# Gate and value products of a conv-FFN by seven Strassen products, residual added by DMA

## The chip, the cores and the metric

The kernel runs on one core of one Trainium2 chip. The metric is the time of one execution on the device, in microseconds. Five engines work side by side, each from its own instruction queue: TensorE (PE in the profile, with PEld for its weight loads), VectorE (DVE), ScalarE (ACT), GpSimd (POOL) and SyncE (SP), which here only issues DMAs. Matmuls read their operands from SBUF and write PSUM; DVE and ACT bring PSUM back into SBUF.

## The reference

One transformer layer on 512 latent tokens and 256 context tokens, model width 2048. Two attention mixers, a residual, and then the channel mixer, which is what the change touches:

```python
def _conv_ffn(h, w_up, conv_w, conv_b, w_down):
    g, u = jnp.split(h @ w_up, 2, axis=-1)
    T = g.shape[1]
    pad = CONV_W // 2
    gp = jnp.pad(g, ((0, 0), (pad, pad), (0, 0)))
    g = sum(gp[:, j:j + T] * conv_w[j] for j in range(CONV_W)) + conv_b
    return (jax.nn.silu(g) * u) @ w_down
...
        x = x + g1 * (_merge_heads(o_da, o_mla, subln_w[l], lambda_init) @ w_o[l])

        h2 = _modulate(_rmsnorm(x, norm2_w[l]), sh2, s2)
        x = x + g2 * _conv_ffn(h2, w_up[l], conv_w[l], conv_b[l], w_down[l])
...
    return _rmsnorm(x, final_w)
```

`w_up` is 2048 x 11264 (gate and value, 5632 columns each), `w_down` 5632 x 2048. Everything is float32; the convolution runs over three neighbouring tokens.

## The kernel before

Tensors lie transposed: features on the 128 partitions, tokens along the free dimension. A float32 product is made of three matmuls in the fast `float32r` format: each operand is split into a high part (a cast on ACT, L75) and a low part (a subtraction on DVE, L76), and `mm3` (L96) multiplies high by high, high by low and low by high (L99, L100, L101), all added up in PSUM. `wblock` (L82) loads a 128 x 1024 block of weights (512 KB, issued by SP, three buffers) and splits it, also into three buffers each for the high and the low part.

The order of the work on each engine is set by a planner: it walks the program with modelled costs, and on each engine issues the earliest instruction of the program whose inputs it takes as ready. So a later instruction may stand ahead of an earlier one that still waits. The engines then run their queues strictly in that order.

The channel mixer comes after the output projection, whose last part builds `x1`, the residual stream, as 16 tiles of 128 features x 512 tokens (L700). `token_norm` (L666) gives the reciprocal root mean square, and a loop over the 16 tiles (L710 to L717) normalises, modulates and splits them into `hx`, 16 pairs of a high and a low tile.

The 5632 gate columns make 44 tiles of 128, and so do the value columns. A *pair* here is one gate tile with the value tile of the same number; its result is 128 x 512 tokens each, for 16 k-tiles of 128.

- `first_pair` computes pairs 0 and 1 together (L723), so that each normalised tile can be used as soon as it is ready: 16 k-tiles x 4 outputs x 3 matmuls of 512 columns. Its four outputs fill both `s` tiles of PSUM (each 128 x 1024, two banks).
- `up(ft)` computes one pair in one `s` tile (L736): four weight blocks of 8 k-tiles each, 96 matmuls of 512 columns.
- `activate` (L747) takes the gate through the convolution (one ACT operation with the middle weight and the bias, two DVE operations for the neighbours), SiLU on ACT, the product with the value on DVE, and the split of the result.
- `down` (L762) multiplies four activation tiles (a *chunk*) with `w_down`: eight weight blocks, 16 output tiles of 12 matmuls each in `b` tiles of PSUM (four of one bank), and DVE multiplies each output by its modulation and adds it to `x1` in SBUF (L771).

The eleven chunks run in this order: pairs of chunk c, then down of chunk c - 1. The last down runs in two halves of 256 tokens, because the final norm of the first half can start while PE works on the second. The final norm and the stores of the output end the kernel.

Of the kernel before, what the change touches and what calls it, by code (L numbers as in the profile page):

```python
# [9 lines left out]
F32 = mybir.dt.float32  # L10
F32R = mybir.dt.float32r
BF16 = mybir.dt.bfloat16
AF = mybir.ActivationFunctionType
# [4 lines left out]
P = 128  # L18
# [31 lines left out]
def layer_kernel(ctx: ExitStack, tc: tile.TileContext, small, rope, c_row, cc_row, x_t, ctx_t, ada, ada_k,  # L50
# [51 lines left out]


    sm = ctx.enter_context(tc.tile_pool(name="sm", bufs=1))
    sm.tile([P, 96], F32, name="edge")
    rim = ctx.enter_context(tc.tile_pool(name="rim", bufs=1, side="right"))
    rim.tile([P, 120], F32, name="rim")


    smt = cst.tile([P, NSMALL], F32, name="smt")  # L110
# [2 lines left out]
    def col(name, j=0):  # L113
        o = OFF[name] + j
        return smt[:, o:o + 1]

    ropet = cst.tile([P, 2, T], F32, name="ropet")
# [14 lines left out]
    q0_d = dram.tile([2, P, T], F32, name="q0_d")  # L132
    cq_d = [dram.tile([2, P, T], F32, name=f"cq_d{i}") for i in range(3)]
    ckv_d = [dram.tile([2, P, TT], F32, name=f"ckv_d{i}") for i in range(2)]
    o_d = [dram.tile([P, T], F32, name=f"o_d{h}") for h in range(NH)]
    kr_d = dram.tile([2, P, TT], F32, name="kr_d")
    k_d = [dram.tile([2, P, TT], F32, name=f"k_d{h}") for h in range(NH)]
# [32 lines left out]
    def a2k(dt=F32):  # L170
        return ap_.tile([P, 512], dt, tag="a2k", name=nm("a2k"))
# [423 lines left out]
    mb = None  # L595
    nxt = latent_pair(0)
    da.release()
    bp = ctx.enter_context(tc.tile_pool(name="bp", bufs=16, reuse_waits="tile"))

    def b2k(dt=F32):  # L600
        return bp.tile([P, 512], dt, tag="b2k", name=nm("b2k"))
# [38 lines left out]
    mb.release()  # L640
    ma.release()
    mc.release()
    ps_b.release()
    ps_b = ctx.enter_context(tc.tile_pool(name="ps_c", bufs=4, space=PSUM, reuse_waits="tile"))


    ap_ = tc.alloc_tile_pool(name="ap2", bufs=32, side="right", reuse_waits="tile")
    wo = tc.alloc_tile_pool(name="wo", bufs=1, reuse_waits="tile")
    cb = wo.tile([P, D], F32, name="cb2")
# [16 lines left out]
    def token_norm(pool, ss, last):  # L666

        n = ss.shape[1]
        po = b_tile()[:, :n]
        pe.matmul(po, ones32, ss, start=True, stop=False)  # L670
        for i, x in enumerate(last):
            q = pool.tile([P, T], F32, tag="sq", name=nm("sq"), bufs=2)[:, :n]
            sc.square(q, x)
            pe.matmul(po, ones32, q, start=False, stop=i == len(last) - 1)
        r, t1, t2 = (pool.tile([P, T], F32, tag=g, name=nm(g), bufs=1)[:, :n] for g in ("nr", "n1", "n2"))
        rstd(r, po, D, t1, t2)
        return r

# [29 lines left out]
    r = token_norm(wo, ss, x1[12:])  # L708
    hx = []
    for dt in range(KT):  # L710
        t = wo.tile([P, T], F32, tag="xr", name=nm("xn"), bufs=3)
        ve.tensor_tensor(t, x1[dt], r, op=ALU.mult)
        h = wo.tile([P, T], F32, tag="h", name=nm("h"), bufs=2)
        sc.activation(h, t, AF.Identity, scale=a2[:, dt:dt + 1], bias=modx[:, 48 + dt:49 + dt])
        hl = a2k(F32R), a2k(F32R)
        split(hl[0], hl[1], h)
        hx.append(hl)  # L717
    wo.release()


    ff = tc.alloc_tile_pool(name="ff", bufs=1, reuse_waits="tile")

    def first_pair():  # L723
# [12 lines left out]
    def up(ft):  # L736
        s = s_tile()
        for i in range(2):
            o = s[:, i * 512:(i + 1) * 512]
            for hf in range(2):  # L740
                wh, wl = wblock(w_up[ft - 2, i, hf])
                for j in range(8):
                    kt = hf * 8 + j
                    mm3(o, (wh[:, j * P:(j + 1) * P], wl[:, j * P:(j + 1) * P]), hx[kt], kt == 0, kt == KT - 1)
        return activate(ft, s)

    def activate(ft, s):  # L747
        g, u = s[:, :512], s[:, 512:]
        t = ff.tile([P, T], F32, tag="t", name=nm("t"), bufs=2)
        sc.activation(t, g, AF.Identity, scale=col("cw", NFT + ft), bias=col("cb", ft))  # L750
        ve.scalar_tensor_tensor(out=t[:, 1:], in0=g[:, :T - 1], scalar=col("cw", ft), in1=t[:, 1:],
                                op0=ALU.mult, op1=ALU.add)
        ve.scalar_tensor_tensor(out=t[:, :T - 1], in0=g[:, 1:], scalar=col("cw", 2 * NFT + ft), in1=t[:, :T - 1],
                                op0=ALU.mult, op1=ALU.add)
        sc.activation(t, t, AF.Silu)
        a = ff.tile([P, T], F32, tag="sq", name=nm("a"), bufs=2)
        ve.tensor_tensor(a, t, u, op=ALU.mult)
        hl = [ff.tile([P, T], F32R, tag=g_, name=nm(g_), bufs=6) for g_ in ("ah", "al")]
        split(hl[0], hl[1], a)
        return hl  # L760

    def down(c, acts, ts=slice(0, T), then=None):  # L762
        for dp in range(8):
            wh, wl = wblock(w_dn[c, dp])
            for i in range(2):
                dt = dp * 2 + i
                po = b_tile()[:, :ts.stop - ts.start]
# [3 lines left out]
                ve.scalar_tensor_tensor(out=x1[dt][:, ts], in0=po, scalar=modx[:, 80 + dt:81 + dt],  # L771
                                        in1=x1[dt][:, ts], op0=ALU.mult, op1=ALU.add)
                if then:
                    then(dt)

    acts = first_pair() + [up(ft) for ft in range(2, FC)]
    for c in range(1, NFC):
        nxt = [up(c * FC + f) for f in range(FC)]
        down(c - 1, acts)
        acts = nxt  # L780


    norms = []
    for th in range(2):
        ts = slice(th * 256, (th + 1) * 256)
        ss = ff.tile([P, 256], F32, tag="ss", name=nm("ss"), bufs=2)
        down(NFC - 1, acts, ts, lambda dt: add_square(ff, ss, x1[dt][:, ts], dt == 0) if dt < 12 else None)
        norms.append(ss)
    exp_ln_tables()
    for th in range(2):  # L790
        ts = slice(th * 256, (th + 1) * 256)
        r = token_norm(ff, norms[th], [x[:, ts] for x in x1[12:]])
        for dt in range(KT):
            y = a2k()[:, :256]
            ve.scalar_tensor_tensor(out=y, in0=x1[dt][:, ts], scalar=col("fw", dt), in1=r, op0=ALU.mult, op1=ALU.mult)
            nc.sync.dma_start(out_t[dt][:, ts], y)
    ff.release()
    ap_.release()


# [77 lines left out]
```

## Time and profile before

| | |
|---|---|
| median of 3 runs | 2536.55 us (2535.35 to 2545.0) |
| profiled execution, its own time | 2537.23 us |
| span of the profile (first to last instruction) | 2535.5 us |
| mean granted TensorE clock | 0.989 |
| busy: PE, PEld, DVE, ACT, POOL | 97%, 79%, 54%, 32%, 4% |
| matmuls | 11852 |
| DMA | 356.94 MB, mean 141 GB/s |

Columns of the profile: "busy" is the time in which an engine had an instruction under way; matmuls are pipelined, so the mean duration of one (392 ns for 512 columns) is longer than the distance between the starts of two, and the distance is what counts. "Idle before, releaser" is the time in which the engine waited just before such an instruction, and the instruction that ended the wait. A row of a timeline has the start in us, the duration in us, the engine, the line and the operation. "Granted clock" is the share of the full TensorE clock that was given. Operands are named by the program's names without their numbers.

### The profile page before, as it was taken

The page shows a single profiled execution, that of the slowest core. Times are in us where ns is not written, and L with a number is a line of the kernel's source. Part 1 is how long each engine was busy: PE and PEld are TensorE (multiplying, and loading weights), DVE is VectorE, ACT ScalarE, POOL GpSimd, SP SyncE. Part 2 cuts the span into 40 slices and gives each one's busy share as a digit, 9 for nine tenths or more (in the row PEclk, how much of TensorE's full clock was granted, in tenths as well). Part 3 has the DMA queues.
Part 4 walks back from the last instruction along what each step waited for, and adds up shares of the span by engine and source line. Part 5 has one row for each costly group of instructions (what it writes and reads, how often), then busy time and mean ns, then how long its engine had stood idle before and what let it go on. Part 6 is the DMA issues. An engine that isn't in the chain of part 4 may idle for free.

```text
span 2535.5 us, 29404 instructions
## 1 busy us (share of the span) xinstructions
PE 2457.9 (97%) x11852; PEld 2003.8 (79%) x11852; DVE 1368.1 (54%) x1779; ACT 820.6 (32%) x1189; POOL 97.7 (4%) x90
## 2 busy tenths in 40 slices
PE   7999999999899999899999999999999999999996
PEld 3778887777777788778888888888888888888886
DVE  4778876498787875533444434343434343434356
ACT  4342221265555622432222222222222222222223
POOL 0000000221100012000000000000000000000003
PEclk9999999999999999999999999999999999999998
DMA  7868898544211185223323223323323333233234
GB/s 276 286 220 320 325 333 307 173 136 135 89 58 55 49 314 197 84 85 99 100 92 100 100 92 100 99 93 100 98 93 100 95 96 100 94 98 100 93 102 146
DMA packets 105214, 356.94 MB, mean 141 GB/s; under 512 B 11379, under 2 KB 22131, under 8 KB 96627
## 3 DMA queue, kind: packets, MB, share of 16 engines
q1 hardware_dynamic: 104118, 351.92, 41.7%
q0 software_dynamic: 960, 3.15, 0.3%
q8 instruction: 93, 1.52, 0.2%
q14 instruction: 43, 0.35, 0.0%
HBM read 331.68 MB, written 23.34 MB: 140 GB/s over the span
## 4 chain that ended last, share of the span: by engine, by line
PE 90%; DVE 6%; ACT 2%; POOL 1%; issue 1%; DMA 1%; DVEq 0%; ACTq 0%; POOLq 0%
PE s L99 16%; PE s L100 16%; PE s L101 16%; PE b L100 10%; PE b L99 10%; PE b L101 10%; PE s L475 3%; PE f L99 1%; PE pt L487 1%; PE f L100 1%; DVE m L477 1%; PE f L101 1%; DVE p L533 1%; PE b L212 1%; PE po L99 1%; POOL p L532 1%
## 5 line engine op out<-in xcount | busy, mean ns | idle before, releaser
L76 DVE TENSOR_TENSOR wl<-wr,wh 128x1024 fp32r<-128x1024 f32 (+2 forms) x382 | 458.8, 1201 | 724.8 <-ACT wh L75 712.9
L75 ACT CAST wh<-wr 128x1024 fp32r<-128x1024 f32 (+2 forms) x382 | 394.3, 1032 | 1142.2 <-PE s L100 668.7
L99 PE MATMUL s<-a2k,wh 128*128 128x512 f32 x1600 | 625.9, 392 | 15.2 <-ACT a2k L75 6.4
L100 PE MATMUL s<-a2k,wh 128*128 128x512 f32 x1600 | 625.9, 391 | 0.0
L101 PE MATMUL s<-a2k,wl 128*128 128x512 f32 x1600 | 625.6, 391 | 0.0
L99 PEld LDWEIGHTS s<-a2k,wh 128*128 128x128 f32 x1600 | 301.4, 189 | 79.2 <-ACT a2k L75 7.6
L100 PEld LDWEIGHTS s<-a2k,wh 128*128 128x128 f32 x1600 | 301.6, 189 | 62.2 <-issue 1.2
L101 PEld LDWEIGHTS s<-a2k,wl 128*128 128x128 f32 x1600 | 301.5, 188 | 62.3 <-issue 0.6
L100 PE MATMUL b<-al,wh 128*128 128x512 f32 (+1 forms) x768 | 285.2, 371 | 0.0
L101 PE MATMUL b<-ah,wl 128*128 128x512 f32 (+1 forms) x768 | 285.2, 371 | 0.0
L99 PE MATMUL b<-ah,wh 128*128 128x512 f32 (+1 forms) x768 | 285.2, 371 | 0.0
L771 DVE SCALAR_TENSOR_TENSOR b2k<-b,modx,b2k 128x512 f32<-128x512 f32 (+1 forms) x192 | 135.1, 705 | 169.0 <-PE b L101 168.7
L164 DVE CUSTOM_DVE_ANT_0 ada<-ada,cb,smt 128x2048 f32<-128x2048 f32 x64 | 151.4, 2368 | 45.6 <-DMA ada<-in_ada 45.4
L100 PEld LDWEIGHTS b<-al,wh 128*128 128x128 f32 x768 | 144.7, 188 | 25.0
L101 PEld LDWEIGHTS b<-ah,wl 128*128 128x128 f32 x768 | 144.7, 188 | 24.9
L99 PEld LDWEIGHTS b<-ah,wh 128*128 128x128 f32 x768 | 144.7, 188 | 24.9
L99 PE MATMUL b<-a2k,wh 128*128 128x512 f32 x304 | 119.7, 394 | 1.6 <-ACT wh L75 1.6
L100 PE MATMUL b<-a2k,wh 128*128 128x512 f32 x304 | 119.5, 393 | 0.0
L101 PE MATMUL b<-a2k,wl 128*128 128x512 f32 x304 | 118.5, 390 | 0.0
L664 POOL TENSOR_TENSOR ss<-ss,sq 128x256 f32<-128x256 f32 (+1 forms) x33 | 45.2, 1371 | 1764.0 <-ACT sq L663 1762.9
L477 DVE TENSOR_REDUCE m<-s 128x1 f32<-128x768 f32 x96 | 90.5, 950 | 15.6 <-PE s L475 15.3
L76 DVE TENSOR_TENSOR wtl<-pt,wth 128x512 fp32r<-128x512 f32 x92 | 63.2, 687 | 20.8 <-ACT wth L75 20.1
(250 smaller groups left out, 2963.7 us busy)
## 6 DMA issues: line engine op xcount, KB each, us to landing
wr<-in_w_up SPq DMA_DIRECT2D x176, 512.0 KB, 3.4
ada<-in_ada SPq DMA_DIRECT2D x64, 1024.0 KB, 6.0
wr<-in_w_dn SPq DMA_DIRECT2D x96, 512.0 KB, 3.4
wr<-in_w_f SPq DMA_DIRECT2D x34, 512.0 KB, 6.4
adak<-in_ada_k SPq DMA_DIRECT2D x32, 512.0 KB, 6.7
ada<-in_ada SPq DMA_DIRECT2D x32, 512.0 KB, 6.8
wr<-in_w_o SPq DMA_DIRECT2D x32, 512.0 KB, 3.5
wr<-in_w_v SPq DMA_DIRECT2D x16, 512.0 KB, 6.8
```

Of the source, the lines that this page charges most:

```text
L75: sc.copy(dst_h, src)
L76: ve.tensor_tensor(dst_l, src, dst_h.bitcast(F32), op=ALU.subtract)
L99: pe.matmul(out, st[0], mv[0], start=start, stop=False, **kw)
L100: pe.matmul(out, st[0], mv[1], start=False, stop=False, **kw)
L101: pe.matmul(out, st[1], mv[0], start=False, stop=stop, **kw)
L164: ve.tensor_tensor_reduce(out=junk, in0=w, in1=vec, op0=ALU.mult, op1=ALU.add, scale=1.0, scalar=col("b_ada", j), accum_out=dst[:, j:j + 1])
L212: pe.matmul(acc[32 * c:32 * c + 32, :n], cpad[:, kt], src(kt), start=j == 0, stop=j == 3)
L475: pe.matmul(s[:, c0:c1], a, b[:, c0:c1], start=i == 0, stop=i == len(mms) - 1)
L477: ve.tensor_reduce(out=m, in_=s[:, :TT], axis=AX.X, op=ALU.max, negate=True)
L487: pe.transpose(pt[:, qt * P:(qt + 1) * P], ws[qt][:, kt * P:(kt + 1) * P], ident)
L664: gp.tensor_tensor(out=ss, in0=ss, in1=q, op=ALU.add)
L771: ve.scalar_tensor_tensor(out=x1[dt][:, ts], in0=po, scalar=modx[:, 80 + dt:81 + dt], in1=x1[dt][:, ts], op0=ALU.mult, op1=ALU.add)
```

## The change

**Products.** For tiles 3 to 43 the product of one pair is done by seven half-size products in place of eight. The two rows of blocks are gate and value weights (W11 and W12 are gate and value for k-tiles 0 to 7, W21 and W22 for k-tiles 8 to 15); the columns are the two halves of the tokens. Four sums of the activations' blocks (`t1` to `t4`) are made once, while they are normalised; four sums of the weights' blocks are made for every pair, on DVE. Each product is 8 k-tiles x 3 matmuls of 256 columns. Three accumulators (`y`, `z`, `x`) of 256 columns lie in one `s` tile; partial sums are copied out by ACT (`m1`, `u2`, `m5`) and the last additions are made by DVE into `g` and `u`. Pairs 0 to 2 stay classical, with the first eight k-tiles held as two halves, so each of their matmuls there becomes two of 256 columns. Pairs 0 and 1 now write `b` tiles.

**Order.** From pair 2 to the last pair the order of PE, ACT, DVE and SP is written out: a list of jobs (weight blocks with their matmuls), with the eight down jobs of the chunk before at fixed places among the 28 products of a chunk; each step runs job i, makes a weight sum, casts job i + 2, does ACT's and DVE's work for job i - 1, and the low part of job i + 2. `Ring` issues the next weight load when a buffer's last use has been written.

**Residual.** `x1` is stored to DRAM tile by tile in the output projection, by POOL. In the down jobs of chunks 0 to 9 ACT multiplies the output by the modulation into one of two buffers `xs`, and a POOL DMA adds it to the DRAM tile. The last down loads the 16 tiles back and adds to them on DVE as before.

Memory pools move to make room (`ropet`, `tp`, `hp`, `mm`, `fin`).

```diff
+DOWN_AFTER = (7, 8, 10, 11, 13, 14, 16, 17)
+XS = 2
...
             x1.append(x)
+            gp.dma_start(x1_d[dt], x)
             if g < 3:
                 add_square(wo, ss, x, dt == 0)
...
+    def normed(kt):
+        b = modx[:, 48 + kt:49 + kt]
+        h = hf[kt] = hp.tile([P, T], F32, tag="h", name=nm("h"), bufs=5)
+        ve.scalar_tensor_tensor(out=h, in0=x1[kt], scalar=a2[:, kt:kt + 1], in1=r, op0=ALU.mult, op1=ALU.mult)
...
+        for (hh, hl), c in parts:
+            sc.activation(hh, h[:, c], AF.Identity, bias=b)
+            ve.scalar_tensor_tensor(out=hl, in0=h[:, c], scalar=b, in1=hh.bitcast(F32), op0=ALU.add, op1=ALU.subtract)
...
+    def sums(j):
...
+        def put_away(t, src):
+            t[j] = half(a2k(F32R) if t is t1 else spare.pop(0) if spare else b2k(F32R))
+            split(t[j][0], t[j][1], src)
+
+        ve.scalar_tensor_tensor(out=d1, in0=c[:, h1], scalar=db[:, j:j + 1], in1=a[:, h1], op0=ALU.add, op1=ALU.add)
+        ve.scalar_tensor_tensor(out=d2, in0=d1, scalar=modx[:, 48 + j:49 + j], in1=a[:, h0], op0=ALU.subtract,
+                                op1=ALU.subtract)
+        put_away(t1, d1)
+        ve.tensor_tensor(d1, a[:, h0], a[:, h1], op=ALU.subtract)
+        put_away(t3, d1)
+        ve.scalar_tensor_tensor(out=d1, in0=c[:, h0], scalar=b, in1=d2, op0=ALU.add, op1=ALU.subtract)
+        put_away(t2, d2)
+        put_away(t4, d1)
+
+    def classical(out, kt, w, start, stop):
+        if kt < 8:
+            mm3(out[:, h0], w, h11[kt], start, False, True)
+            mm3(out[:, h1], w, h12[kt], False, False, True)
+        else:
+            mm3(out, w, h2[kt], False, stop, True)
 
     def first_pair():
-        ss_ = [s_tile(), s_tile()]
-        for kb in range(8):
+        outs = [b_tile() for _ in range(4)]
+        order = [kb for j in range(4) for kb in (j, j + 4)]
+        for n_, kb in enumerate(order):
             wh, wl = wblock(w_up0[kb])
             for j in range(2):
                 kt = kb * 2 + j
+                normed(kt)
+                if n_ and n_ % 2 == 0:
+                    sums(n_ - 2 + j)
                 for i in range(4):
                     o = j * 512 + i * P
-                    mm3(ss_[i // 2][:, (i % 2) * 512:(i % 2 + 1) * 512], (wh[:, o:o + P], wl[:, o:o + P]), hx[kt],
-                        kt == 0, kt == KT - 1)
-        return [activate(ft, s) for ft, s in enumerate(ss_)]
+                    classical(outs[i], kt, (wh[:, o:o + P], wl[:, o:o + P]), kt == 0, kt == KT - 1)
+        for j in (6, 7):
+            sums(j)
+        return [activate(ft, outs[2 * ft], outs[2 * ft + 1]) for ft in range(2)]
...
-    acts = first_pair() + [up(ft) for ft in range(2, FC)]
-    for c in range(1, NFC):
-        nxt = [up(c * FC + f) for f in range(FC)]
-        down(c - 1, acts)
-        acts = nxt
...
+    with tc.manual_schedule(engines={mybir.EngineType.PE, mybir.EngineType.Activation, mybir.EngineType.DVE,
+                                     mybir.EngineType.SP}):
+        ra, rb = Ring(wp, "wr", 3, items_a), Ring(mm, "rb", 3, items_b)
...
+        def weight_sum(ft, i):
...
+            if i == 1:
+                ve.tensor_tensor(sums_[ft, 1], w12, ra.tiles["w11", ft], op=ALU.subtract)
+                ra.used(("w11", ft))
+            elif i == 2:
+                ve.tensor_tensor(sums_[ft, 2], w22, sums_[ft, 1], op=ALU.subtract)
+                rb.used(("w22", ft))
+            elif i == 3:
+                ve.tensor_tensor(w12, w22, w12, op=ALU.subtract)
+                rb.used(("w12", ft))
+                rb.used(("w22", ft))
+            else:
+                ve.tensor_tensor(sums_[ft, 2], w21, sums_[ft, 2], op=ALU.subtract)
+                rb.used(("w21", ft))
...
+                hs, out, start = ((h11, "y", True), (h21, "x", True), (t2, "y", False), (t1, "z", False),
+                                  (t3, "y", False), (t4, "z", False), (h22, "y", False))[k]
+                for j in range(8):
+                    mm3(live[ft][out], w[j], hs[j], start and j == 0, j == 7, True)
...
+        def act_after(i):
...
+            elif job[0] == "d":
+                for d, po in enumerate(live["po"]):
+                    dt = job[2] * 2 + d
+                    x = mm.tile([P, T], F32, tag="xs", name=nm("xs"), bufs=XS)
+                    sc.mul(x, po, modx[:, 80 + dt:81 + dt])
+                    gp.dma_start(x1_d[dt], x, accum_op=ALU.add)
+            elif job[0] == "p":
+                ft, k = job[1:]
+                v = live[ft]
+                if k == 0:
+                    v["m1"] = small("m1")
+                    sc.copy(v["m1"], v["y"])
+                elif k == 2:
+                    v["u2"] = small("u2")
+                    sc.copy(v["u2"], v["y"])
+                elif k == 3:
+                    v["m5"] = small("m5")
+                    sc.copy(v["m5"], v["z"])
+                elif k == 6:
+                    sc.copy(v["g"][:, h1], v["y"])
+                    v["t"] = gate_in(ft, v["g"])
...
+            if k == 2 and f:
+                silu(convolve(ft - 1, f["g"], f["t"]))
+            elif k == 3:
+                if f:
+                    acts[ft - 1] = multiply(f["t"], f["u"])
+                v["g"] = mm.tile([P, T], F32, tag="g", name=nm("g"), bufs=1)
+                ve.tensor_tensor(v["g"][:, h0], v["x"], v["m1"], op=ALU.add)
+            elif k == 4:
+                if f:
+                    finish(f["t"], acts[ft - 1])
+                v["u"] = mm.tile([P, T], F32, tag="u", name=nm("u"), bufs=1)
+                ve.tensor_tensor(v["u"][:, h1], v["y"], v["m5"], op=ALU.add)
+            elif k == 5:
+                ve.tensor_tensor(v["u"][:, h0], v["z"], v["u2"], op=ALU.add)
...
+        for i, job in enumerate(jobs):
+            run(i)
+            if job[0] == "p":
+                ft, k = job[1:]
+                if k in (0, 1, 2):
+                    weight_sum(ft, k + 2)
+                elif k == 6:
+                    weight_sum(ft + 1, 1)
+            elif job == ("u", 3):
+                weight_sum(3, 1)
+            cast(i + 2)
+            if i:
+                act_after(i - 1)
+                vec_after(i - 1)
+            low(i + 2)
```

More of the change, by code (lines that the diff above doesn't have):

```diff
@@ L707, in layer_kernel @@
                                 in1=col("n2", dt), op0=ALU.add, op1=ALU.mult)
[L708 to L717, printed above, removed]
+    db = sm.tile([P, 8], F32, name="db")
@@ L754, in activate, with silu, multiply, finish @@
                                 op0=ALU.mult, op1=ALU.add)
+        return t
+    def silu(t):
         sc.activation(t, t, AF.Silu)
[L756 to L759, printed above, removed]
-        return hl
-    def down(c, acts, ts=slice(0, T), then=None):
+        return t
+    def multiply(t, u):
+        ve.tensor_tensor(t, t, u, op=ALU.mult)
+        hl = [ff.tile([P, T], F32R, tag=g_, name=nm(g_), bufs=5) for g_ in ("ah", "al")]
+        sc.copy(hl[0], t)
+        return hl
+    def finish(t, hl):
+        ve.tensor_tensor(hl[1], t, hl[0].bitcast(F32), op=ALU.subtract)
+        return hl
+    def down(c, acts, ts, dst, then):
         for dp in range(8):
@@ new lines, in down, with __init__, pump, used @@
+                then(dt)
+    acts = {}
+    for ft, a in enumerate(first_pair()):
+        acts[ft] = a
+    hp.release()
+    mm = tc.alloc_tile_pool(name="mm", bufs=1, side="right", reuse_waits="tile")
+    PAIRS = range(3, NFT)
+    h21, h22 = ([tuple(p[:, c] for p in h2[8 + j]) for j in range(8)] for c in (h0, h1))
+    class Ring:
+        def __init__(self, pool, tag, bufs, items):
+            self.pool, self.tag, self.bufs, self.items = pool, tag, bufs, items
+            self.tiles, self.left, self.n = {}, {}, 0
+            self.pump()
+        def pump(self):
+            while self.n < len(self.items):
+                if self.n >= self.bufs and self.left[self.items[self.n - self.bufs][0]]:
+                    return
+                key, src, uses = self.items[self.n]
+                t = self.pool.tile([P, 1024], F32, tag=self.tag, name=nm(self.tag), bufs=self.bufs)
+                nc.sync.dma_start(t, src)
+                self.tiles[key], self.left[key] = t, uses
+                self.n += 1
+        def used(self, key):
+            self.left[key] -= 1
+            self.pump()
@@ new lines, in layer_kernel @@
+    jobs = [("u", b) for b in range(4)]
+    for ft in PAIRS:
+        for k in range(7):
+            jobs.append(("p", ft, k))
+            c, n_ = ft // FC, (ft % FC) * 7 + k
+            if c and n_ in DOWN_AFTER:
+                jobs.append(("d", c - 1, DOWN_AFTER.index(n_)))
+    last = len(jobs)
+    items_a, items_b = [], []
+    for job in jobs:
+        if job[0] == "u":
+            items_a.append((job, w_up[0, job[1] // 2, job[1] % 2], 1))
+        elif job[0] == "d":
+            items_a.append((job, w_dn[job[1], job[2]], 1))
+        elif job[2] == 0:
+            ft = job[1]
+            items_a.append((("w11", ft), w_up[ft - 2, 0, 0], 2))
+            items_b += [(("w12", ft), w_up[ft - 2, 1, 0], 2), (("w21", ft), w_up[ft - 2, 0, 1], 2),
+                        (("w22", ft), w_up[ft - 2, 1, 1], 3)]
@@ L783, in layer_kernel @@
+    mm.release()
+    fin = tc.alloc_tile_pool(name="fin", bufs=1, side="right", reuse_waits="tile")
+    x1 = [a2k() for _ in range(KT)]
     norms = []
     for th in range(2):
-        ts = slice(th * 256, (th + 1) * 256)
-        ss = ff.tile([P, 256], F32, tag="ss", name=nm("ss"), bufs=2)
-        down(NFC - 1, acts, ts, lambda dt: add_square(ff, ss, x1[dt][:, ts], dt == 0) if dt < 12 else None)
+        ts = slice(th * HT, (th + 1) * HT)
+        ss = fin.tile([P, HT], F32, tag="ss", name=nm("ss"), bufs=2)
+        down(NFC - 1, [acts[NFT - FC + f] for f in range(FC)], ts, x1,
+             lambda dt: add_square(fin, ss, x1[dt][:, ts], dt == 0) if dt < 12 else None)
```

149 lines of the change are left out of this document (124 added, 25 removed).

## Prediction

> **What bounds the kernel now.** I read the page's engine sums and chain of waits first, then busy time by stretch, then single matmuls in the timeline.
>
> ```profile
> PE 2457.9 (97%) x11852; PEld 2003.8 (79%) x11852; DVE 1368.1 (54%) x1779; ACT 820.6 (32%) x1189; POOL 97.7 (4%) x90
> ...
> PE 90%; DVE 6%; ACT 2%; POOL 1%; issue 1%; DMA 1%; DVEq 0%; ACTq 0%; POOLq 0%
> ```
>
> TensorE holds 90% of the chain that ended last. By stretch (window, length, busy time and instructions of PE, PEld, DVE, ACT, POOL, granted clock, DMA share, GB/s):
>
> ```profile
> 1070.00:1075.00 5.00, 5.00 (x24) 4.14 (x23) 4.82 (x8) 4.93 (x8) 0.00 (x0) 1.00 0.14 33
> 1107.00:1112.00 5.00, 1.35 (x6) 0.77 (x5) 4.08 (x6) 4.42 (x5) 0.00 (x0) 0.94 0.25 87
> 1112.00:1117.00 5.00, 4.32 (x10) 3.45 (x11) 2.60 (x4) 1.84 (x3) 0.00 (x0) 0.50 0.25 92
> 1122.00:2464.50 1342.50, 1342.50 (x5924) 1111.66 (x5923) 536.80 (x574) 338.55 (x373) 0.00 (x0) 1.00 0.30 97
> 2464.50:2510.60 46.10, 46.10 (x386) 46.07 (x385) 31.81 (x47) 24.48 (x41) 23.94 (x22) 1.00 0.39 126
> ```
>
> From 1122 to 2464.5 us, the gate, value and down products, PE has no gap while DVE works 40% of the time. Only fewer matmul microseconds help there. One matmul of 512 columns takes 1342.50 / 5924 = 0.2266 us. The last down, in halves of 256 columns, gives the other price; the timeline's start times are
>
> ```profile
> 1112.68 0.79 PE L99 MATMUL s<-a2k,wh 128*128 128x512 f32 x1 [4.32 <-DVE a L757]
> ...
> 1117.96 0.54 PE L99 MATMUL s<-a2k,wh 128*128 128x512 f32 x1
> ...
> 2464.52 0.28 PE L99 MATMUL b<-ah,wh 128*128 128x256 f32 x1
> ...
> 2510.48 0.28 PE L101 MATMUL b<-ah,wl 128*128 128x256 f32 x1
> ```
>
> ```profile
> L99 PE MATMUL b<-ah,wh 128*128 128x256 f32 x128 | 36.2, 283 | 0.0
> ```
>
> L99, L100 and L101 have 128 each, 384 in all: (2510.48 - 2464.52) / 383 = 0.1200 us. So half the columns cost 53%, not 50%, and PEld is busy 46.07 of 46.10 us. The first two rows show what a stop costs: after 4.32 us of idle the granted clock is 0.50, and the 12 matmuls from 1112.68 to 1117.96 take 5.28 us instead of 2.72, so 2.6 us more.
>
> **The change, part by part. Products on PE.** A pair was 96 matmuls of 512: 96 x 0.2266 = 21.76 us. It becomes seven products of 24 matmuls of 256: 168 x 0.1200 = 20.16 us. The gain is 1.60 us a pair and, over 41 pairs, 65.4 us. It is 7%, not an eighth, because of the 53%. The Trainium skill (TensorE: Matmul & The Clock Gate, Back-to-back issue gap) gives N / 2.4 + 2.5 ns between warm matmuls, thus 0.109 and 0.216 us; by it the gain would be 41 x (96 x 0.216 - 168 x 0.109) = 99 us. The trace's 0.1200 and 0.2266 disagree with it and decide.
>
> The classical tile 2 splits its first eight k-tiles in two halves: 24 x (2 x 0.1200 - 0.2266) = 0.32 us for each of two outputs, so +0.6 us. Down products are the same matmuls, 0.
>
> **Does PE stay fed?** Durations by operation and shape (busy, mean ns):
>
> ```profile
> L76 DVE TENSOR_TENSOR wl<-wr,wh 128x1024 fp32r<-128x1024 f32 x358 | 439.7, 1228 | 720.3 <-ACT wh L75 708.6 <-PE s L101 3.3
> L75 ACT CAST wh<-wr 128x1024 fp32r<-128x1024 f32 x358 | 377.3, 1054 | 1135.6 <-PE s L100 668.7 <-PE b L100 344.8 <-PE b L101 82.6
> L76 DVE TENSOR_TENSOR mvl<-f,mvh 128x256 fp32r<-128x256 f32 x24 | 10.0, 422 | 4.2 <-ACT mvh L75 3.9
> L75 ACT CAST mvh<-f 128x256 fp32r<-128x256 f32 x24 | 9.0, 374 | 11.3 <-PE f L101 11.1
> L326 DVE SCALAR_TENSOR_TENSOR c2k<-h,modc,c2k 128x256 fp32r<-128x256 f32 x16 | 7.7, 480 | 0.6 <-ACT c2k L325 0.6
> L326 DVE SCALAR_TENSOR_TENSOR a2k<-h,modx,a2k 128x512 fp32r<-128x512 f32 x16 | 12.0, 750 | 5.7 <-ACT a2k L325 5.7
> L750 ACT ACTIVATE t<-s,smt 128x512 f32<-128x512 f32 x44 | 34.1, 776 | 3.3 <-PE s L101 3.3
> L753 DVE SCALAR_TENSOR_TENSOR t<-s,smt,t 128x511 f32<-128x511 f32 x44 | 32.9, 748 | 1.2
> L755 ACT ACTIVATE t<-t 128x512 f32<-128x512 f32 x44 | 27.8, 633 | 95.6 <-DVE t L753 95.6
> L757 DVE TENSOR_TENSOR a<-t,s 128x512 f32<-128x512 f32 x44 | 30.3, 688 | 32.3 <-ACT t L755 32.2
> L75 ACT CAST ah<-a 128x512 fp32r<-128x512 f32 x44 | 27.4, 623 | 43.0 <-PE b L101 25.7 <-DVE a L757 16.8
> L76 DVE TENSOR_TENSOR al<-a,ah 128x512 fp32r<-128x512 f32 x44 | 30.3, 692 | 21.1 <-ACT ah L75 21.0
> ```
>
> DVE for a pair: seven low parts (8.60 us), four weight sums priced as the same shape (4.91), two convolution steps (1.50), multiply and low part of the activation (1.38), three additions of 256 at 0.48 (1.44): 17.8 us. In a pair's first job the sum (L76's shape, 1.23) stands before the cast that reads it (1.05), so DVE waits 1.05 us more: 18.9 of 20.16 us. ACT: seven casts, four copies of 256, gate, SiLU, activation cast: 7.38 + 1.50 + 2.03 = 10.9 us. The order works two jobs ahead, so low parts have 2 x 2.88 us to arrive. 17 of the 28 products of four pairs run with no down job between; the others add 5.44 us of PE to at most 1.23 us of DVE. Added waits: a cast may wait for a sum, the SiLU for the convolution, a PSUM accumulation for the copy before it. Latest is the first product's copy: ACT's queue until it is the cast that waits for the sum, the last tile's copy and gate, the next cast and the copy, 1.23 + 1.05 + 0.37 + 0.78 + 1.05 + 0.37 = 4.85 us into the pair, and the accumulation behind it starts at 5.76. SP's order is written out too; behind a load that waits for its buffer stand all later ones.
>
> ```profile
> wr<-in_w_up SPq DMA_DIRECT2D x176, 512.0 KB, 3.4
> ```
>
> A pair's W12 buffer is freed by a low part in its third job, by 8.6 us, and the next pair's W12 is read from 17.3 on: 8.6 us for the 3.4 us of that row, and the next three loads have about the same. I cost the feed at 0. If DVE's 18.9 were exceeded by over 1.3 us, PE would wait: that is rival A.
>
> **First two tiles.** The sums of the moving operand (3 scalar operations, one subtraction, 4 splits for each of 8 k-tile pairs) now stand among the normalisation, and five h buffers hold that order.
>
> ```profile
> 1052.93 1.22 DVE L76 TENSOR_TENSOR wl<-wr,wh 128x1024 fp32r<-128x1024 f32 x1
> ...
> 1059.40 3.10 DVE L712 TENSOR_TENSOR xn<-b2k,nr 128x512 f32<-128x512 f32 x5
> ...
> 1108.63 0.75 DVE L753 SCALAR_TENSOR_TENSOR t<-s,smt,t 128x511 f32<-128x511 f32 x1
> 1109.30 1.22 DVE L76 TENSOR_TENSOR wl<-wr,wh 128x1024 fp32r<-128x1024 f32 x1
> 1110.43 0.75 DVE L751 SCALAR_TENSOR_TENSOR t<-s,smt,t 128x511 f32<-128x511 f32 x1
> ```
>
> DVE starts at 1059.40 with at most three blocks split before. Up to the last normalised tile it has 8 x (0.75 + 2 x 0.48) + 8 x 1.50 = 25.7, six sums of 3 x 0.48 + 5 x 0.42 = 3.54, thus 21.2, and five low parts, 6.1: 53.0 us, to 1112.4. The last block's 24 matmuls (5.44) follow the tile before, at 1110.9, to 1116.3; two sums (7.1) and the next low part (1.2) end at 1120.7, where before the next tile began at 1112.68. The clock is paid in both: +8.0. Lower end: operations overlap as those at 1059.40 (five in 3.10 us, not 3.45), 93 of them by 0.07 us, DVE is done at 1105.9, PE at 1109.8, and the next tile follows without a stop: -2.9 - 2.6 = -5.5. Upper end: strict order, with 0.6 us for each of 16 ACT hand-overs and 0.8 in eight sums, and both activations (2 x 2.9) before the low part: 9.6 + 6.4 + 5.8 more, +29.8. I take +8, since 4.82 of 5.00 us in 1070 to 1075 show DVE and ACT interleaved, not waiting.
>
> **The end.** Tile 43's activation was covered by a whole down; now the last down needs it at once: copy 0.37, gate 0.78, convolution 1.50, SiLU 0.63, multiply 0.69, cast 0.62, low 0.69 = 5.3 us. Four outputs of nine matmuls not using it cover 4.3, if PE's order has them first: 1.0; else 5.3 + 2.6 (clock) = 7.9. The low part at 1109.30, of a later block, stands between the convolutions of tiles 0 and 1, so the planner does fill gaps on DVE; no row shows PE. I take the middle, 4.4. The reloads:
>
> ```profile
> xr<-in_x_t SPq DMA_DIRECT2D x16, 256.0 KB, 3.9
> ...
> GB/s 276 286 220 320 325 333 307 173 136 135 89 58 55 49 314 197 84 85 99 100 92 100 100 92 100 99 93 100 98 93 100 95 96 100 94 98 100 93 102 146
> ```
>
> Sixteen of 256 KB and eight blocks of 512 KB, less three blocks loaded early, are 6.8 MB in 23.0 us, 296 GB/s under the 333 that a slice reached; 3.9 us is less than four outputs take (5.8). 0, or +5 if they queue.
>
> **Residual.** DVE loses 160 additions; ACT gains 160 multiplications of 0.78, hidden in 5.44-us down jobs; POOL issues 176 DMAs, 16 of them stores in the output projection, where PE covers them. The two xs buffers are the new wait (rival B). 0.
>
> **Sum** against the profiled execution's 2537.23: -65.4 + 0.6 + 8.0 + 4.4 = -52.4, 2485. That run is 0.7 us above the median shown.
>
> **Rivals. A: DVE becomes the bound of the products.** Its 18 operations a pair each cost 0.15 us more in hand-overs: 21.6 us, 1.4 over PE's pair. In 17 products in a row that is 3.4 us, over ten stretches 34: 2519, or 2502 at half that. For it: 94% of the pair by my sum. Against: overlap as above.
>
> **B: the accumulating DMAs hold ACT.** The rows nearest are POOL's stores of before:
>
> ```profile
> L463 POOL DMA_DIRECT2D v_d<-kl x6: 752/752/763, 473.0 to 488.1; - x6
> DMA to landing us min/median/max: 2.7/6.0/12.2
> ...
> v_d<-kl POOLq DMA_DIRECT2D x6, 256.0 KB, 7.3
> ```
>
> The multiplication of a down output waits until the DMA two outputs earlier has left its buffer; behind it in ACT's queue stand the casts, and PE waits for them. Seven steps between a chunk's down jobs take 4 x 8.32 + 3 x 11.20 = 66.9 us, 9.55 each. With landing time L, ACT falls behind by 7 x (0.78 + L - 9.55) a chunk, less 5.8 us of lead, ten times. It eats the 52 us from L = 10.3; at the row's 12.2 it costs 182: 2667, slower. For it: these DMAs also read DRAM. Against: the median is 6.0 over all stores to v_d and 7.3 for this POOL half, so I place L near 7, below 9.55 - 0.78 = 8.8, where nothing is held. The Trainium skill (SBUF — State Buffer, SBUF: two separate sides) says that a DMA issued from GpSimd starves for descriptors while DVE holds the shared port in a two-port mode, and the section after it gives 620 ns growing to about 3100; 2.5 us on 7.3 makes 9.8 by estimate, just below 10.3, so by that rule B comes near. POOL's issues of 752 to 763 ns show no such wait.
>
> **C: the change doesn't do what it says**, every job's first matmul waiting 0.15 us for its low part: 371 jobs, 56 us, 2541, no gain. Against: no PE gap from 1122 on at the same hand-over.
>
> **Chances.** Forecast 0.72 (own range 2468 to 2505), A 0.13, B 0.10, C 0.05. Half a percent, 12.7 us, is about what a measurement can tell. Faster 0.72 + 0.13 = 0.85, same 0.05, slower 0.10. The range, 2466 to 2516, holds forecast and most of A.
>
> **What would show it.** Matmul starts 0.120 us apart in the products with PE idle near 0 right; DVE idle before PE's waits right for the forecast, DVE busy over 95% in down-free stretches for A; ACT's multiplications waiting on the DMA for B. The start of tile 2 at about 1121 and a gap of 1 to 8 us before the last down test the two losses. Spacing above 0.125, or PE waits spread over the products, would make it wrong.

## The result and the profile after

The changed kernel takes 2563.8 us (median; 2557.82 to 2566.73), the kernel before on the same chip 2536.91 us: a ratio of 1.0097, 95% interval 1.0067 to 1.0126. It is 27 us slower where 52 us less was forecast. Its profiled execution took 2557.82 us, span 2556.0, 20.6 us more than the profiled one of before.

The page of the changed kernel, engine sums and chain of waits:

```profile
PE 2420.2 (95%) x14948; PEld 2104.7 (82%) x14948; DVE 1643.2 (64%) x2102; ACT 1087.3 (43%) x1660; POOL 245.3 (10%) x266
...
PE 82%; DVE 8%; ACT 5%; issue 1%; DMA 1%; POOL 1%; SPq 0%; ACTq 0%; DVEq 0%; POOLq 0%
```

Neither DVE nor ACT is full, but the share of TensorE in the chain fell from 90% to 82%, and theirs rose from 8% to 13%. From the first product of tile 3 to the last one of tile 43 (window, length, busy time and instructions of PE, PEld, DVE, ACT, POOL, clock, DMA share, GB/s):

```profile
1137.60:2482.30 1344.70, 1288.24 (x8818) 1192.64 (x8817) 777.78 (x815) 598.60 (x813) 139.69 (x160) 1.00 0.51 129
```

Before, TensorE was busy for the whole of such a stretch; now 56 us of it are empty, at a granted clock of 1.00. What TensorE waited for from 1050 to 2540 us (rows of 1 us and more; total us, times, longest):

```profile
PE s L102 <- DVE g L1028: 18.4, 20, 0.9
PE s L102 <- DVE u L1033: 16.4, 30, 0.6
PE s L102 <- ACT m L999: 10.8, 21, 0.5
PE s L102 <- ACT u L1002: 9.7, 21, 0.5
PE b L102 <- ACT a2k L749: 5.0, 1, 5.0
PE s L102 <- ACT wh L945: 4.4, 1, 4.4
PE b L102 <- ACT ah L824: 2.6, 1, 2.6
PE b L682 <- ACT sq L681: 1.5, 2, 0.9
PE b L102 <- ACT wh L78: 1.1, 1, 1.1
```

The first four rows are the loss: 92 waits in the products, always for one of four operations that read an accumulator in PSUM. Lines are those of the changed kernel: L999 copies m1, L1002 u2, L1028 adds to g, L1033 to u. They stand in front of products k = 2, 4, 5 and 6 of a pair, and only where no down block is near. One of them in the timeline of TensorE:

```profile
1278.98 0.28 PE L102 MATMUL s<-a2k,wh 128*128 128x256 f32 x1
...
1281.74 0.28 PE L104 MATMUL s<-a2k,wl 128*128 128x256 f32 x1
1282.48 0.39 PE L102 MATMUL s<-tp,wh 128*128 128x256 f32 x1 [0.46 <-ACT u L1002]
1282.70 0.28 PE L103 MATMUL s<-tp,wh 128*128 128x256 f32 x1
```

and ACT at the same time:

```profile
1279.06 1.06 ACT L945 CAST wh<-rb 128x1024 fp32r<-128x1024 f32 x1 [1.95 <-PE s L103]
1282.05 0.37 ACT L1002 COPY u<-s 128x256 f32<-128x256 f32 x1 [1.94 <-PE s L104]
```

Product k = 3 starts at 1278.98 (24 matmuls back from 1281.74) and writes z. The copy reads y, which k = 2 had finished by then. ACT is idle for 1.94 us and still does not copy; it starts right behind the last matmul of k = 3, and k = 4, which writes y again, starts behind the copy. The reader waits for a product whose output it doesn't read. The add to g (L1028) costs most, 1.2 us for each stop from start to start against 0.7 to 0.8, since it also stands behind the copy m5, which waits in this way for k = 4.

A stop costs more than its bracket says. 1281.74 to 1282.48 is 0.74 us where 0.12 is normal, so 0.62, though the row says 0.46 (a matmul is drawn 0.28 us long); the next start is 0.22 behind, 0.10 more. The four rows' 55.3 us become 55.3 + 92 x 0.26 = 79.2 us, and the sum over all 92 stops from start to start is 79.2 us too. That is more than the 65.4 us that the products were to gain.

### The profile page after: what moved, and what is told of

It reads as the page before. It is cut to its first block, busy times and chain, and to the rows that moved or that the text cites. A ratio compares the mean times of both kernels' runs of the same rounds, so it can differ in the third digit from the quotient of the medians.

```text
span 2556.0 us, 37051 instructions
## 1 busy us (share of the span) xinstructions
PE 2420.2 (95%) x14948; PEld 2104.7 (82%) x14948; DVE 1643.2 (64%) x2102; ACT 1087.3 (43%) x1660; POOL 245.3 (10%) x266
## 4 chain that ended last, share of the span: by engine, by line
PE 82%; DVE 8%; ACT 5%; issue 1%; DMA 1%; POOL 1%; SPq 0%; ACTq 0%; DVEq 0%; POOLq 0%
PE s L102 14%; PE s L103 13%; PE s L104 13%; PE b L103 10%; PE b L102 10%; PE b L104 10%; PE s L480 2%; ACT wh L945 2%; PE f L102 1%; PE pt L492 1%; DVE m L482 1%; PE f L103 1%; PE f L104 1%; DVE p L538 1%; PE b L217 1%
## 5 line engine op out<-in xcount | busy, mean ns | idle before, releaser
L102 PE MATMUL s<-a2k,wh 128*128 128x256 f32 (+1 forms) x1536 | 461.3, 301 | 24.9 <-DVE u L1033 16.4
L103 PE MATMUL s<-a2k,wh 128*128 128x256 f32 (+1 forms) x1536 | 458.9, 299 | 0.0
L104 PE MATMUL s<-a2k,wl 128*128 128x256 f32 (+1 forms) x1536 | 458.9, 299 | 0.0
L993 POOL DMA_DIRECT2D x_d<-xs x160 | 139.7, 1001 | 1258.9 <-ACT xs L992 1256.9
L78 ACT CAST wh<-wr 128x1024 fp32r<-128x1024 f32 (+2 forms) x134 | 132.7, 991 | 268.6 <-PE b L104 84.4
L951 DVE TENSOR_TENSOR wl<-ws,wh 128x1024 fp32r<-128x1024 f32 x123 | 150.4, 1223 | 136.6 <-ACT wh L945 136.6
L79 DVE TENSOR_TENSOR wl<-wr,wh 128x1024 fp32r<-128x1024 f32 (+2 forms) x134 | 156.6, 1169 | 104.3 <-ACT wh L78 100.7
L951 DVE TENSOR_TENSOR wl<-wr,wh 128x1024 fp32r<-128x1024 f32 x125 | 151.7, 1220 | 110.7 <-ACT wh L945 110.5
L951 DVE TENSOR_TENSOR wl<-rb,wh 128x1024 fp32r<-128x1024 f32 x123 | 150.1, 1221 | 96.8 <-ACT wh L945 96.8
L103 PE MATMUL s<-b2k,wh 128*128 128x256 f32 x656 | 185.6, 283 | 0.0
L102 PE MATMUL s<-b2k,wh 128*128 128x256 f32 x656 | 185.6, 283 | 0.0
L104 PE MATMUL s<-b2k,wl 128*128 128x256 f32 x656 | 185.4, 283 | 0.0
```

The costliest lines, as they stand in the source:

```text
L78: sc.copy(dst_h, src)
L79: ve.tensor_tensor(dst_l, src, dst_h.bitcast(F32), op=ALU.subtract)
L102: pe.matmul(out, st[0], mv[0], start=start, stop=False, **kw)
L103: pe.matmul(out, st[0], mv[1], start=False, stop=False, **kw)
L104: pe.matmul(out, st[1], mv[0], start=False, stop=stop, **kw)
L951: ve.tensor_tensor(lo, raw, hi.bitcast(F32), op=ALU.subtract)
```

## The experiments

### One tile or two for the accumulators, and SP's order

Theory A says that a reader waits for the last write to the *tile* it reads from, whatever columns. y, z and x are column ranges of one tile of two banks, and the readers of product k stand in the order behind product k + 1, so that each waits for k + 1 and k + 2 waits for it. B says that readers are late behind other work, C that a switch of accumulator has a price. (These are theories on the result; the prediction's rivals A, B and C are others.)

e1_split gives y a tile, and z and x together another; the two buffers of each fill the same four banks, with y in a bank of its own as before. The pool of the `s` tiles is closed and opened again for this. (Tile 2's gate and value, the classical blocks, get a tile each too.)

```diff
+    def yz():
+        return [ps_s.tile([P, 512], F32, tag=g, name=nm(g)) for g in ("y", "zx")]
...
-                    s = s_tile()
-                    live[ft] = {"y": s[:, :HT], "z": s[:, 512:512 + HT], "x": s[:, 512 + HT:]}
+                    y, zx = yz()
+                    live[ft] = {"y": y[:, :HT], "z": zx[:, :HT], "x": zx[:, HT:]}
```

> The seven products' three accumulators, until now column ranges of one PSUM tile of two banks, become two tiles of one bank each (y in one; z and x in the other); the two buffers of each fill the same four banks, and the order on every engine stays as it was. Theory A (a reader of an accumulator waits for the last write to its tile, which is the last matmul of the product after it, and the second product after it then waits for the reader): every product pair of TensorE waits gets a whole product (24 x 0.12 = 2.88 us) as cover, so the 94 waits of TensorE in the products (20 on the add to g of mean 1.08 us, 21 on the copy m1 of 0.68, 21 on the copy u2 of 0.62, 30 on the add to u of 0.71, all measured as the gap between starts) go to nearly none: 70 to 80 us off the changed kernel's 2563.8, thus 2484 to 2494, faster than the kernel before. Theory B (the copies and adds come late because ScalarE and VectorE have other work queued ahead of them): the queues are the same, so the waits stay, 2550 to 2564. Theory C (a switch from one accumulator to another costs TensorE something by itself): as B, 2555 to 2564.

(The four counts make 92, not 94.)

e2_ring leaves the accumulators and makes the ring of the seven-product weights later, so that SP issues the loads of tile 2's blocks first:

```diff
-        ra, rb = Ring(wp, "wr", 3, items_a), Ring(mm, "rb", 3, items_b)
+        ra = Ring(wp, "wr", 3, items_a)
...
         low(1)
+        rb = Ring(mm, "rb", 3, items_b)
```

> The changed kernel with only the ring of the seven-product weights made later, after the first two blocks are cast, so that the fourth classical block of tile 2 (u3) is loaded ahead of the ring's first three blocks on SP's queue. Theory: TensorE's 4.39 us of idle time at 1125.57 comes from u3's load standing behind the ring's loads, which wait for the tiles of the sums to be freed at 1120; with it goes the half-clocked stretch of about 2 us behind it: 5 to 7 us off 2563.8, thus 2557 to 2559, and the products start that much earlier. Rival (VectorE's sums and casts of that stretch set the time): 0 to 1 us, 2563 to 2564.

e3_both has both edits.

> Both edits together. If both theories hold they add, since the one acts before the first product and the other within the products: 2478 to 2488, the fastest of all. If theory A of the split holds and the queue's does not, as the split alone.

Against 2537.03 us for the kernel before in the same runs:

| kernel | median us (range) | ratio to before, 95% interval |
|---|---|---|
| e1_split | 2477.77 (2475.05 to 2478.5) | 0.9761 (0.9748 to 0.9774) |
| e2_ring | 2555.25 (2551.98 to 2560.28) | 1.0069 (1.0054 to 1.0084) |
| e3_both | 2470.63 (2467.39 to 2474.92) | 0.9736 (0.9720 to 0.9751) |

e1_split takes 86 us off the changed kernel by the medians and 83 between the profiled executions (2557.82 and 2475.05), somewhat more than A's 70 to 80; B and C, with 2550 and more, are out. Its two stretches, products and last down:

```profile
1137.43:2400.78 1263.35, 1263.35 (x8810) 1186.68 (x8808) 781.90 (x816) 600.09 (x813) 139.76 (x160) 1.00 0.54 138
2400.78:2449.10 48.32, 46.77 (x387) 46.30 (x386) 33.36 (x49) 27.48 (x47) 24.48 (x22) 1.00 0.40 132
```

With the same instructions, DVE's and ACT's included, 81 us went out of the products (the 79.2, and 2 us because a stop of 1.06 us and nine matmuls of the last down no longer fall between them) and TensorE is full. What TensorE waited for in the whole kernel behind 1050 us is now (rows of 1 us and more; two others have 0.2 us each, ahead of the products):

```profile
PE b L102 <- ACT a2k L749: 5.0, 1, 5.0
PE zx L102 <- ACT wh L951: 4.1, 1, 4.1
PE b L102 <- ACT ah L824: 1.6, 1, 1.6
PE b L682 <- ACT sq L681: 1.5, 2, 0.9
```

All 92 are gone. With the same four banks the waits are not there: the tile called for them, not the bank. The copy u2 (L1008 here) no longer idles for TensorE but follows the cast ahead of it:

```profile
1239.38 1.05 ACT L951 CAST wh<-wr 128x1024 fp32r<-128x1024 f32 x1 [1.83 <-PE y L103]
1240.34 0.37 ACT L1008 COPY u<-y 128x256 f32<-128x256 f32 x1
```

The second row of the waits, TensorE on a cast in tile 2, is what e2_ring and e3_both are about. In the changed kernel the queue of SP reads

```profile
1096.81 0.33 SPq L869 DMA_DIRECT2D wr<-in_w_up  x1
1120.07 1.28 SPq L869 DMA_DIRECT2D rb<-in_w_up  x3
1121.40 10.40 SPq L869 DMA_DIRECT2D wr<-in_w_up  x4
```

and in e3_both

```profile
1098.11 10.40 SPq L875 DMA_DIRECT2D wr<-in_w_up  x2
1118.50 1.28 SPq L875 DMA_DIRECT2D rb<-in_w_up  x3
1119.88 1.85 SPq L875 DMA_DIRECT2D wr<-in_w_up  x2
```

Three loads of the ring had to wait until 1120.07 for the temporary tiles from which `t1` to `t4` are made (`SPq L869 <- DVE d L769`, 22.9 us), and tile 2's last block stood behind them. From the first pair's first matmul to the first product it was 1060.79 to 1137.60, 76.8 us, in the changed kernel; in e3_both it is 70.2 (1059.61 to 1129.77), and there is no such wait. Over this stretch the edit is worth 6.1 us alone (70.7 in e2_ring) and 6.3 with the split (76.5 in e1_split), inside the 5 to 7 expected; by the medians it is 8.6 and 7.1. e3_both beats both kernels: 66 us, 2.6%, under the one before.

### The same operations in other places

e4_slots and e5_places keep the one tile and move the down blocks. In e4_slots two stand next to each other:

```diff
-DOWN_AFTER = (7, 8, 10, 11, 13, 14, 16, 17)
+DOWN_AFTER = (6, 6, 8, 8, 13, 13, 15, 15)
```

> The changed kernel with its accumulators in one tile as they were, and only the places of the eight down blocks within each 28 products moved: from behind products 7, 8, 10, 11, 13, 14, 16, 17 to two behind each of 6, 8, 13, 15. No operation is added or removed. Theory A: a wait is hidden only where a down block, which writes other banks, stands between a product and the second after it; seven of the sixteen places of 28 products were covered so and now two are, so ten times (k=4 twice, k=5 twice, k=6 once) come back, 20 x 0.62 + 20 x 1.08 + 10 x 0.71 = 41 us and about 0.1 us more for each of the 50: 2604 to 2611. Theory B (readers late behind other work on their engines) and C (a fixed price for a switch): the same work in another place, 2558 to 2572; C not above 2566.

It took 2638.99 us (2633.89 to 2641.55), and is no test: of two neighbours, both sets of copies read the second block's outputs, so that the first one's are left out, and they wait for the second block as well. That adds waits of ScalarE which A does not speak of. Its counts of TensorE's waits are still those of A: 40 on the add to g, 41 on u2, 21 on m1, 40 on the add to u. e5_places has a product between any two:

```diff
-DOWN_AFTER = (7, 8, 10, 11, 13, 14, 16, 17)
+DOWN_AFTER = (5, 6, 7, 8, 12, 13, 14, 15)
```

> The changed kernel with its accumulators in one tile, and only the eight down blocks of each 28 products moved, from behind products 7, 8, 10, 11, 13, 14, 16, 17 to behind 5, 6, 7, 8, 12, 13, 14, 15, with at least one product between any two; the same operations. Theory A (readers wait for the last write to their tile): a wait in front of k=2, 4, 5 or 6 is hidden only where a down block stands on one of the two places ahead of it. Seven of sixteen were hidden, now four are: of 28 products k=4 and k=5 each come back twice and k=6 goes once, so over ten chunks 20 x 0.62 + 20 x 1.08 - 10 x 0.71 = 27 us and about 0.1 us for each of 30 more waits: 2563.8 + 30, 2590 to 2597. Theory B (readers late behind other work on their engines) or C (a fixed price of a switch): 2558 to 2570.

2590.49 us (2588.36 to 2594.47), ratio 1.0204 (1.0188 to 1.0219): 26.7 us more than the changed kernel (27 by the ratios, each against the kernel before in the same runs). TensorE's waits in the products:

```profile
PE s L102 <- DVE g L1028: 36.8, 40, 0.9
PE s L102 <- ACT u L1002: 18.9, 41, 0.5
PE s L102 <- ACT m L999: 10.6, 21, 0.5
PE s L102 <- DVE u L1033: 10.3, 20, 0.5
```

A's rule gives the counts exactly: 20 + 20, 21 + 20, 21, and 30 - 10. The length of each wait is as before; only how many are covered has changed. B and C expected no change.

### What the other steps were worth

e6_noacc and e7_dve start from e3_both. e6_noacc stores the down outputs without adding them in DRAM:

```diff
-                    gp.dma_start(x1_d[dt], x, accum_op=ALU.add)
+                    gp.dma_start(x1_d[dt], x)
```

> The fastest kernel so far (split accumulators and later ring, 2470.6) with the down blocks' DMAs storing without adding, so that the output holds only the last two chunks and no residual: this leaves out the addition in DRAM alone. If the adding DMAs cost nothing on the path (the forecast's step, at 0): 2467 to 2475. If they hold ScalarE's buffers or the weight loads (rival B), it becomes faster by more than 5 us, below 2466.

2473.68 us (2472.15 to 2477.23), ratio 0.9744 (0.9729 to 0.9758): no gain. POOL's DMAs in e3_both (issue time of one in ns, minimum, median and maximum; median us to landing):

```profile
L999 POOL DMA_DIRECT2D x_d<-xs x160: 850/862/1234, 1180.3 to 2368.2; - x160
...
x_d<-xs POOLq DMA_DIRECT2D x160, 256.0 KB, 5.9
```

and in e6_noacc:

```profile
L999 POOL DMA_DIRECT2D x_d<-xs x160: 540/540/552, 1185.2 to 2374.4; - x160
...
x_d<-xs POOLq DMA_DIRECT2D x160, 256.0 KB, 2.5
```

An adding DMA lands in 5.9 us where the storing one takes 2.5, and its issue is 0.3 us longer; nothing on the path waits for either.

e7_dve repeats weight sums, four more operations a pair on VectorE:

```diff
                 ve.tensor_tensor(sums_[ft, 1], w12, ra.tiles["w11", ft], op=ALU.subtract)
+                ve.tensor_tensor(sums_[ft, 1], w12, ra.tiles["w11", ft], op=ALU.subtract)
...
                 ve.tensor_tensor(sums_[ft, 2], w22, sums_[ft, 1], op=ALU.subtract)
+                ve.tensor_tensor(sums_[ft, 2], w22, sums_[ft, 1], op=ALU.subtract)
...
                 ve.tensor_tensor(w12, w22, w12, op=ALU.subtract)
+                ve.tensor_tensor(w12, w22, w12, op=ALU.subtract)
+                ve.tensor_tensor(w12, w22, w12, op=ALU.subtract)
```

> The fastest kernel so far (2470.6) with VectorE loaded more: of the weight sums of a pair the first two are made twice and the third three times, four operations of 1.22 us more a pair, 4.9 us. By the prediction's price of VectorE (18.9 of 20.16 us a pair with hand-overs) it now needs 23.8 us; in the 17 products without a down block, 49.0 us of TensorE, that is 57.8, late by 8.8 us, of which the two blocks of lead hide 5.8: TensorE waits 3 to 9 us in each of ten chunks, 2500 to 2560. If the margin was larger than the prediction's sum says, since operations overlap and hand-overs are hidden by the lead: 2468 to 2485. It shows how near rival A was; the values stay the same but for rounding.

2520.65 us (2516.39 to 2526.16), ratio 0.9930 (0.9908 to 0.9953): 50 us above e3_both. Its products, and what TensorE waits for in them:

```profile
1133.50:2443.57 1310.07, 1279.05 (x8809) 1189.77 (x8808) 969.32 (x979) 593.29 (x813) 139.71 (x160) 1.00 0.52 133
```

```profile
PE y L102 <- ACT m L1009: 16.1, 21, 1.2
PE zx L104 <- DVE wl L961: 8.3, 21, 1.2
PE zx L102 <- DVE g L1038: 6.6, 20, 0.3
```

The stretch is 46.7 us longer than in e1_split, 4.7 us for each of ten chunks, inside the 3 to 9 expected. The first row names ScalarE, but the casts ahead of its copy m1 wait for VectorE's sums (`ACT wh L955 <- DVE ws L927`, 53.2 us in ten waits). VectorE is busy for 74% of the products and yet decides, since it is short only where no down block stands. One such run of products (there are 18 in a row; the prediction counts 17), in e1_split and in e7_dve:

```profile
1377.43:1429.26 51.83, 51.83 (x433) 51.83 (x432) 41.84 (x45) 27.04 (x36) 1.75 (x2) 1.00 0.41 121
1381.90:1438.28 56.38, 53.35 (x434) 52.13 (x433) 51.35 (x54) 26.39 (x36) 1.75 (x2) 1.00 0.37 104
```

In e1_split VectorE is busy for 81% of it, where the prediction's sum gave 88%, 94% with hand-overs, and no wait is left; in e7_dve it is 91%, and the run is 4.6 us longer. The prediction's rival A was not what happened, but its place was right: 24% more VectorE work makes it real.

## Why the prediction was wrong

**Products on PE, -65.4: right.** In e1_split, free of gaps, 6888 matmuls of 256 columns at 0.1200 us and 1920 of 512 at 0.2266 make 1261.6 us; the stretch took 1263.35. By the same rates 41 classical pairs and the down blocks would take 1327.0, so 63.7 us were gained.

**Does PE stay fed? This is the step that failed: "I cost the feed at 0".** It cost 79 us. The step took as the latest wait the copy of the first product, at 4.85 us against an accumulation at 5.76, and let each reader start when its own product is done. It added up the work ahead of a reader in its queue, but did not ask which matmul the reader waits for. With one tile that is the last matmul of the *next* product, and the cover of a whole product, 2.88 us, which the alternation of y, z and x was to give, is nothing. The prediction's own sign of being wrong, "PE waits spread over the products", is what came. The mechanism is shown three times: ACT idle for 1.94 us ahead of a copy whose operand is ready, all 92 waits gone with the tile split and every operation the same, and the counts of e5_places. Not one of the three rivals names it. C, a small wait in many jobs, has the nearest form, but put it on the low parts, at 0.15 us for each of 371 jobs; it is 0.86 us (79.2 / 92) at 92 places.

The Trainium skill (Perfetto Trace Analysis, Matmuls) asks for independent matmul groups to rotate through different PSUM banks, so that reading one overlaps the next group's matmuls. The changed kernel does that by bank, y in one and z and x in the other, and its trace does not overlap: the rule holds here only once the banks are also tiles of their own. The same page of the Trainium skill (Perfetto Trace Analysis, Optimization Strategy) says that one gap repeating on the engine that should be full can mean too little SBUF or PSUM for the next tile; here the repeating gap went away in the same four banks.

The trace of before held a hint. Its gate and value outputs are halves of one tile as well; a tile takes 21.76 us, the gate half of it the first 10.9, and counted on from 1137.10, where tile 2 ended, tile 6 ended at 1224.1. ACT in that stretch:

```profile
1218.74 1.06 ACT L75 CAST wh<-wr 128x1024 fp32r<-128x1024 f32 x1 [4.38 <-PE s L100]
1224.18 1.06 ACT L75 CAST wh<-wr 128x1024 fp32r<-128x1024 f32 x1 [4.38 <-PE s L100]
1225.13 0.78 ACT L750 ACTIVATE t<-s,smt 128x512 f32<-128x512 f32 x1
```

The gate's columns were done at about 1213.3, ACT idled twice for 4.38 us, and the operation that reads them alone ran at 1225.13, behind the value's last matmul. The order that was planned for ACT may have caused this too, so it proves nothing; but it was the row to ask about, since a wait there had a whole tile of cover, which the change takes away.

**First two tiles: +8.0 predicted, +1.3 measured; inside the bounds, but the mechanism was another.** Before, the first pair's first matmul and the end of tile 2 are

```profile
1062.21 1.22 PE L99 MATMUL s<-a2k,wh 128*128 128x512 f32 x2 [6.41 <-ACT a2k L75]
```

```profile
1112.68:1137.10 24.42, 24.42 (x96) 20.00 (x97) 5.66 (x6) 4.38 (x6) 0.00 (x0) 0.89 0.26 78
```

thus 74.9 us against 76.8 after, of which 0.6 is tile 2's halves. The step let DVE hold tile 2 back to 1120.7. Tile 2 did not start there: its matmuls stand among the first pair's from 1099.98 on, TensorE is busy for 25.52 us of the 25.59 up to 1125.57, and the stop that the step charged, with its clock, is not there. The stop was elsewhere, at SP. The prediction says of SP that "behind a load that waits for its buffer stand all later ones", and then applies it only to the products, not to the first loads of the ring; that costs about 6 us in

```profile
1125.57 0.28 PE L104 MATMUL s<-h,wl 128*128 128x256 f32 x1
1130.24 0.80 PE L102 MATMUL s<-a2k,wh 128*128 128x512 f32 x1 [4.39 <-ACT wh L945]
```

which e3_both does not have. Its 70.2 us are 4.7 less than before, or 5.3 without the halves, where the step's lower end is 5.5 less. So +1.3 is a gain that the step did not expect and a stop that it did not see, and that the two nearly cancel is luck.

**The end, +4.4: inside its bounds, partly by luck.** From the last product (2482.21) to the last down matmul (2531.67) 49.46 us pass for 375 matmuls that take 45.0 at 0.1200: 4.5, and the 1.06 us of the wait on a cast ahead of it make 5.5. The stop before the activation is the forecast one:

```profile
2488.37 0.95 PE L102 MATMUL b<-ah,wh 128*128 128x256 f32 x4 [2.64 <-ACT ah L824]
```

In e1_split the end costs 2.2 us (48.25 against 384 x 0.1200). There all 36 matmuls that do not use tile 43 stand behind the last product and cover its activation, and the stop is 1.6 us; in the changed kernel nine of them had gone ahead of the last product, and 9 x 0.1200 is the 1.1 us by which its stop is longer. So neither of the step's two cases (1.0 and 7.9) is what the trace shows, and the middle met the sum.

**Residual and reloads, 0: right, and the prediction's rival B is out.** ScalarE waited 1.9 us in all for its xs buffers in the changed kernel, with landings of 5.9 us where 7 was taken and 10.3 would have decided:

```profile
ACT xs L992 <- DMA x_d<-xs: 1.9, 3, 0.9
```

The steps add up as measured: -63.7 + 0.6 + 1.3 + 79.2 + 5.5 is +22.9. Less the 1.4 us by which the first pair started earlier in that execution, and the 0.7 by which the final norm was shorter, it is +20.8, against +20.6 measured. The forecast's own sum of 2485 is met, and passed, by e1_split (2477.77), where the feed is free and the first tiles and the end came about 9 us cheaper than forecast.

## What to carry to other kernels

When an accumulator is to be read while TensorE fills another, work out for each reader *which* matmul releases it, not only how full its engine's queue is: if both accumulators belong to one tile, give them tiles of their own in the same banks. In an order written out by hand, go through every queue from its first instruction on, loads included, and ask of each what it waits for and what stands behind it. Gaps of half a microsecond look small in a page where TensorE is 95% busy; count them from start to start, since 92 of them outweighed a saving of 64 us.

## What was not expected of the hardware

In the same places of the kernel an adding DMA of 256 KB to DRAM lands in 5.9 us, a storing one in 2.5, with 0.86 and 0.54 us to issue it on POOL; the adds of 160 such blocks cost the kernel nothing. A stop of half a microsecond on TensorE leaves the granted clock at 1.00 in the products (the stretch from 1137.60 above), and so does one of 1.6 us at the end of e1_split (the stretch from 2400.78), while behind the stop of 2.64 us at the end it is 0.58 (window, columns as above):

```profile
2488.37:2490.50 2.13, 2.13 (x10) 2.06 (x11) 1.24 (x3) 0.36 (x1) 0.00 (x0) 0.58 0.00 0
```
